# Numpy transposes the first expert matrix, the score keys and the gate matrices before the launch, and the kernel stops transposing them

## The chip, the cores and the metric

The kernel runs on one NeuronCore of a Trainium2 chip. The metric is the device time of one launch in microseconds (us). What numpy does on the host before the launch is not in it. Five engines work beside each other, each in its own fixed order, and wait for one another through semaphores: PE (TensorE: matmuls, and transposes as matmuls against an identity), DVE (VectorE), ACT (ScalarE), POOL (GpSimd) and SP (SyncE, which mostly issues DMAs).

## The reference, cut to what matters

Two layers. Each has a token mixer (attention, mLSTM and a gating MLP side by side) and then a layer of retrieved experts (PEER). There are 512 tokens of width 1024 and 16384 experts per layer.

```python
def spatial_gating(u, v, w_s, b_s):
    ...
    gate = jnp.einsum('gts,bcsgd->bctgd', w_s * tril, v5) + b_s.T[:, :, None]
...
def peer_ffn(xn, wq, sub_keys, u_tab, v_tab):
    q = jnp.matmul(xt, wq).reshape(t, PEER_HEADS, 2, PEER_SUBDIM)
    scores = jnp.einsum('thcd,hcnd->thcn', q, sub_keys)
    sv, si = lax.top_k(scores, PEER_TOPK)
    ...
    best_s, best_p = lax.top_k(cand_s, PEER_TOPK)
    idx = jnp.take_along_axis(cand_i, best_p, axis=-1)
    gate = jax.nn.softmax(best_s, axis=-1)
    ...
        act = jnp.einsum('td,thkd->thk', xb, u_tab[ib])
        wgt = jax.nn.gelu(act) * gb
        return jnp.einsum('thk,thkd->td', wgt, v_tab[ib])
```

`u_tab` and `v_tab` are the kernel's `peer_u` and `peer_v`, [2, 16384, 1024] in float32.

## The kernel before, in words

For the first 384 tokens (TD) the kernel doesn't gather experts. It computes all 16384 activations densely, in 128 blocks of 128 experts: `act = u_block @ x` (`uact`, L733), then gelu, then a product with a sparse gate matrix, then `y += w^T @ v_block` (`vmm`, L989). Each fp32 operand is split into a high and a low fp32r part, and a product is three matmuls (hi*hi, hi*lo, lo*hi). The last 128 tokens are done by gathers: 128 indirect DMAs of rows of `peer_u` and 128 of `peer_v` per layer (`gather_u` L763, `gather_v` L774), each followed by one DVE operation of 128x1024. In these texts a "block" is one such block of 128 experts, and a "gather" is the DVE operation that uses a gathered row.

`uact` needs the block with its 1024 channels on the partitions, but `peer_u` holds it with the experts on them. So each block is loaded (`uload`, L683), transposed and split into `u_hi` (ACT) and `u_lo` (DVE) (`utrans`, L693). There are two ways to transpose. In the first 54 blocks of a layer PE does it: eight 128x128 transposes into two PSUM tiles (L711), each with its own ACT copy (L713) and DVE subtraction (L714) of 128x512. In the other 74 blocks DVE does it: the load comes as four DMAs that place 32-row pieces (L688), one STREAM_TRANSPOSE of 128x1024 finishes it (L702), and ACT and DVE split the whole tile (L705, L706).

A layer runs through these stretches:

- **mixer**, in which four gate matrices are transposed by PE (L550), and **front** (`peer_front`, L618): 16 score projections on PE, each with a key matrix that PE transposes (L648) and ACT copies (L650), and the first top-k on DVE.
- **selection** (`stage2`, L803): the second top-k and the indices of four token tiles on DVE. `paced` (L925) emits a whole block's load, transposes and `uact` for each unit of credit.
- **one-hot** (`onehots`, L895): the sparse gate matrix is built from bf16 one-hot products, DVE 2 `oeq` and 3 `oag` operations per 16 tokens, PE 48 matmuls, ACT four copies. Blocks go on by the same credit, and a gather is emitted at every second step.
- **tail** (L1003 to 1010): 12 blocks and 12 gathers, no other work. Block 51 is its first.
- **dense** (L1014 to 1027): 128 steps of `vmm`, 65 blocks spread between them, the remaining gathers of both kinds.

From the front to the end of the one-hot stretch the Tile scheduler sets the order of each engine when the program is built. The tail and the dense stretch stand in the order in which they are written (`manual_schedule`). The number of blocks in each stretch follows from the credits, which the change doesn't touch: 51 before the tail.

Buffers: three of `u_raw`, two each of `u_hi` and `u_lo`, four for gathered rows, and one PSUM tag `T` with two buffers for the transposes.

## Time and profile before

| | |
|---|---|
| median of 3 runs | 3360.24 us (3348.55 to 3373.12) |
| profiled execution | 3358.58 us, span 3356.9 us, mean granted PE clock 0.986 |
| PE busy | 96% |
| DVE busy | 83% |
| ACT busy | 42% |
| POOL busy | 19% |
| DMA | 742.40 MB, mean 221 GB/s |

The stretches are cut in the trace at these points of layer 0: the front ends when PE has done its last score matmul (L659, 438 us), the one-hot stretch begins with the first `oeq` (L907, 594.1 us) and ends with the last `oag` (L911, 783.8 us), the dense stretch begins with the first `y` matmul (L997, 861 us) and ends with the last (1676.6 us). In layer 1 the same points are 2117.7, 2274.1, 2463.2, 2540.7 and 3352.5 us.

How to read it: a busy share is a mean over a stretch. PE matmuls are pipelined, so a matmul's own duration (341 ns for 384 columns) is longer than the step from its start to the start of the next. What a matmul costs is that step, and it is read from the timeline or from the chain, where a run of equal matmuls has one row with the time to the next piece.

### The profile page before, as it was taken

What the parts mean: (1) busy time and instruction counts of PE and PEld (TensorE: products, weight loads), DVE (VectorE), ACT (ScalarE), POOL (GpSimd) and SP (SyncE); (2) the same over time, 40 slices, a digit from 0 to 9 for tenths busy, and PEclk for the clock granted to TensorE, in tenths of its full rate; (3) what the DMA queues carried; (4) which work ended last, traced back from release to release, by engine and by line L of the source; (5) the groups of instructions that cost most, each with busy time, mean ns of one, the idle gap of its engine ahead of it and who ended that gap; (6) DMA issues with size and microseconds to landing.
All of it is one profiled execution on the core that took longest, in us unless ns stands there. A gap on an engine that the chain in (4) does not pass through costs nothing.

```text
span 3356.9 us, 49064 instructions
## 1 busy us (share of the span) xinstructions
PE 3237.4 (96%) x18400; PEld 2875.2 (86%) x18400; DVE 2792.9 (83%) x4911; ACT 1395.2 (42%) x2142; POOL 652.1 (19%) x563
## 2 busy tenths in 40 slices
PE   8999999999999999999989999999999999999999
PEld 8787899898888888888887778889988888888888
DVE  4757898997888888988847578989978888989888
ACT  4554333664333333333355533336643333333333
POOL 1000003111232232223200000032112222332232
PEclk9999999999999999999999999999999999999999
DMA  4212137777999999999732121377779999999997
GB/s 136 72 33 90 56 121 273 265 282 230 279 296 291 283 292 291 304 297 290 246 112 66 32 90 55 121 271 265 282 233 282 296 289 289 302 301 302 286 290 255
DMA packets 388687, 742.40 MB, mean 221 GB/s; under 512 B 32996, under 2 KB 269600, under 8 KB 385376
## 3 DMA queue, kind: packets, MB, share of 16 engines
q1 hardware_dynamic: 295264, 398.64, 43.1%
q0 software_dynamic: 74752, 269.84, 25.4%
q10 hardware_dynamic: 18432, 70.79, 5.3%
q8 instruction: 144, 2.36, 0.3%
q14 instruction: 95, 0.78, 0.1%
HBM read 666.26 MB, written 72.88 MB: 220 GB/s over the span
## 4 chain that ended last, share of the span: by engine, by line
PE 65%; DVE 13%; DMA 11%; issue 5%; ACT 4%; POOL 1%; SPq 0%; ACTq 0%; DVEq 0%; POOLq 0%
PE y L997 22%; PE act L738 17%; PE mm L187 12%; DMA v_raw<-in_peer_v_dram 8%; PE oh L917 3%; PE mm L533 3%; DVE u_lo L714 2%; DMA u_raw<-in_peer_u_dram 1%; DVE u_t L702 1%; PE T L711 1%; PE zz L367 1%; PE zz L659 1%; PE zz L467 1%; PE y L478 1%; PE y L400 1%
## 5 line engine op out<-in xcount | busy, mean ns | idle before, releaser
L738 PE MATMUL act<-xh,u_lo 128*128 128x384 f32 x2048 | 698.1, 341 | 19.4 <-DVE u_lo L706 19.4
L738 PE MATMUL act<-xh,u_hi 128*128 128x384 f32 x2048 | 705.8, 345 | 11.1 <-ACT u_hi L705 10.7
L738 PE MATMUL act<-xl,u_hi 128*128 128x384 f32 x2048 | 696.7, 340 | 0.0
L997 PE MATMUL y<-v_hi,wh 128*128 128x512 f32 x1536 | 600.0, 391 | 8.8 <-ACT wh L984 8.8
L997 PE MATMUL y<-v_lo,wh 128*128 128x512 f32 x1536 | 600.2, 391 | 1.3 <-DVE v_lo L985 1.2
L997 PE MATMUL y<-v_hi,wl 128*128 128x512 f32 x1536 | 599.2, 390 | 0.0
L983 ACT ACTIVATE v_hi<-v_raw 128x1024 fp32r<-128x1024 f32 x256 | 272.0, 1062 | 742.6 <-DMA v_raw<-in_peer_v_dram 336.0
L985 DVE TENSOR_TENSOR v_lo<-v_raw,v_hi 128x1024 fp32r<-128x1024 f32 x256 | 313.1, 1223 | 146.4 <-ACT v_hi L983 146.2
L738 PEld LDWEIGHTS act<-xh,u_lo 128*128 128x128 f32 x2048 | 388.2, 190 | 26.8 <-DVE u_lo L706 26.8
L738 PEld LDWEIGHTS act<-xh,u_hi 128*128 128x128 f32 x2048 | 388.7, 190 | 24.8 <-ACT u_hi L705 17.3
L738 PEld LDWEIGHTS act<-xl,u_hi 128*128 128x128 f32 x2048 | 388.3, 190 | 4.8
L997 PEld LDWEIGHTS y<-v_hi,wh 128*128 128x128 f32 x1536 | 288.9, 188 | 65.8 <-ACT wh L984 10.7
L997 PEld LDWEIGHTS y<-v_hi,wl 128*128 128x128 f32 x1536 | 289.1, 188 | 62.5 <-DVE wl L986 1.5
L997 PEld LDWEIGHTS y<-v_lo,wh 128*128 128x128 f32 x1536 | 289.0, 188 | 58.0 <-DVE v_lo L985 2.9
L702 DVE STREAM_TRANSPOSE u_t<-u_raw 128x1024 f32<-128x1024 f32 x148 | 327.9, 2215 | 0.1
L765 POOL DMA_INDIRECT rows<-in_peer_u_dram,idx x128 | 150.3, 1174 | 788.1 <-DVE rows L768 412.7
L765 POOL DMA_INDIRECT sbuf<-in_peer_u_dram,idx x128 | 147.8, 1154 | 590.4 <-DVE sbuf L768 468.4
L741 ACT ACTIVATE gelu<-act 128x384 f32<-128x384 f32 x256 | 124.3, 485 | 299.7 <-PE act L738 298.7
L776 POOL DMA_INDIRECT rows<-in_peer_v_dram,idx x128 | 172.4, 1347 | 380.7 <-DVE x_sb L779 355.9
L984 ACT ACTIVATE wh<-wf 128x384 fp32r<-128x384 f32 x256 | 132.7, 518 | 244.9 <-DVE wf L980 244.0
L776 POOL DMA_INDIRECT sbuf<-in_peer_v_dram,idx x128 | 163.5, 1277 | 337.0 <-DVE x_sb L779 313.8
L706 DVE TENSOR_TENSOR u_lo<-u_t,u_hi 128x1024 fp32r<-128x1024 f32 x148 | 181.2, 1224 | 55.5 <-ACT u_hi L705 55.1
(309 smaller groups left out, 5890.1 us busy)
## 6 DMA issues: line engine op xcount, KB each, us to landing
v_raw<-in_peer_v_dram SPq DMA_DIRECT2D x256, 512.0 KB, 12.0
u_raw<-in_peer_u_dram SPq DMA_DIRECT2D x592, 128.0 KB, 11.5
u_raw<-in_peer_u_dram SPq DMA_DIRECT2D x108, 512.0 KB, 4.2
gd<-st ACTq DMA_DIRECT2D x24, 2048.0 KB, 7.3
gt<-gd SPq DMA_DIRECT2D x64, 768.0 KB, 14.0
w_raw<-in_w_in_dram SPq DMA_DIRECT2D x28, 768.0 KB, 4.5
ge<-gelu ACTq DMA_DIRECT2D x104, 192.0 KB, 4.4
gelu_r<-ge SPq DMA_DIRECT2D x104, 192.0 KB, 10.4
```

The lines of the kernel that those rows point to most:

```text
L187: nc.tensor.matmul(ps, a_sel(a[ah], d), b_sel(b[bh], d), start=(d == 0 and i == 0), stop=(d == n - 1 and i == 2))
L533: nc.tensor.matmul(pt, yT[ah][:, b, t * P:(t + 1) * P], wo[bh][:, b, hs], start=(b == 0 and m == 0), stop=(b == n - 1 and m == 2))
L702: nc.vector.transpose(uraw[e].rearrange("p c (g b) -> p g c b", g=4), src.rearrange("p g (f c) -> p g c f", f=32))
L706: nc.vector.tensor_sub(ul, uraw[e], uh.bitcast(F32))
L738: nc.tensor.matmul(pa[:, :TD], a[:, d, :], b[:, d, :TD], start=(d == 0 and i == 0), stop=(d == ND - 1 and i == 2))
L741: nc.scalar.activation(gelu[e], pa[:, :TD], AF.Gelu_apprx_tanh)
L765: nc.gpsimd.indirect_dma_start(out=r, out_offset=None, in_=u_rows, in_offset=bass.IndirectOffsetOnAxis(ap=idx[:, p:p + 1], axis=0))
L776: nc.gpsimd.indirect_dma_start(out=r, out_offset=None, in_=v_rows, in_offset=bass.IndirectOffsetOnAxis(ap=idx[:, p:p + 1], axis=0))
L983: nc.scalar.activation(vh, vraw[e], AF.Copy)
L984: nc.scalar.activation(wh, wf, AF.Copy)
L985: nc.vector.tensor_sub(vl, vraw.pop(e), vh.bitcast(F32))
L997: nc.tensor.matmul(ya[2 * t + half], a[:, tsl], b[:, hs], start=(k == 0 and i == 0), stop=(k == NK - 1 and i == 2))
```

## The change

In `kernel()` numpy makes three arrays before the launch: `sg_w` and `peer_keys` with their last two axes exchanged, in place of the originals, and a new input `peer_ut`, a copy of `peer_u` with each block as [partition f, channel group c, expert n], so that a partition's 1024 values of a block are 4096 contiguous bytes. `peer_u` stays an input, since the gathers read it. In the kernel the identity transposes of blocks, keys and gate matrices go, with the ACT copy of the key. `uload` is one DMA of 512 KB for every block, `utrans` becomes `uprep` (one ACT copy and one DVE subtraction of 128x1024 per block), and the DVE transposes go with the two constants that chose their blocks.

```diff
@@ sg_all
-                    pw = ps.tile([P, S], F32, name="tr", bufs=1)
-                    nc.tensor.transpose(pw[:, :P], wr, ident)
                     wt = tmp("dg", 2, (P, NT, P))[:, 0, :]
-                    nc.vector.tensor_mul(wt, pw[:, :P], upper)
+                    nc.vector.tensor_mul(wt, wr, upper)
@@ peer_front
-                    kr = fr.tile([P, P], F32, name="kr", bufs=2)
-                    nc.sync.dma_start(kr, peer_keys[l, h, which])
-                    pk = ps.tile([P, S], F32, name="zz", bufs=4)
-                    nc.tensor.transpose(pk[:, :P], kr, ident)
-                    kt = fr.tile([P, P], F32, name="kt", bufs=2)
-                    nc.scalar.activation(kt, pk[:, :P], AF.Copy)
+                    kt = fr.tile([P, P], F32, name="kt", bufs=3)
+                    nc.sync.dma_start(kt, peer_keys[l, h, which])
@@ layer
             def uload(e):
-                if e < NK and dve_t(e):
...
-                    for a in range(4):
-                        nc.sync.dma_start(uraw[e][32 * a:32 * (a + 1)], rows[a])
-                elif e < NK:
-                    uraw[e] = pools["up"].tile([P, D], F32, name="u_raw", bufs=3)
-                    nc.sync.dma_start(uraw[e], peer_u[l, e * NK:(e + 1) * NK, :])
-
-            def utrans(e, half, ps, tag="T", **kw):
...
+                if e < NK:
+                    uraw[e] = pools["up"].tile([P, ND, P], F32, name="u_raw", bufs=3)
+                    nc.sync.dma_start(uraw[e], peer_ut[l, e])
+
+            def uprep(e):
+                if e < NK:
+                    uh = pools["up"].tile([P, ND, P], F32R, name="u_hi")
+                    ul = pools["up"].tile([P, ND, P], F32R, name="u_lo")
+                    src = uraw.pop(e)
+                    nc.scalar.activation(uh, src, AF.Copy)
+                    nc.vector.tensor_sub(ul, src, uh.bitcast(F32))
+                    uT[e] = (uh, ul)
@@ uphase
-                utrans(e + 1, 0, ps)
-                utrans(e + 1, 1, ps)
+                uprep(e + 1)
                 uact(e, ps)
@@ tail
-                        utrans(e + 1, 0, ps, f"y{2 * n % 6}")
-                        utrans(e + 1, 1, ps, f"y{(2 * n + 1) % 6}")
+                        uprep(e + 1)
                         gather(G_R)
                         uact(e, ps, bufs=2)
@@ dense
                             uload(eu + 3)
-                            utrans(eu + 1, 0, ps)
                         vprep(k + 1)
                         spread(2 * k, 252)
                         if u_on:
                             uact(eu, ps, bufs=2)
-                            utrans(eu + 1, 1, ps)
+                            uprep(eu + 1)
@@ kernel
+    inputs["sg_w"] = _np.swapaxes(inputs["sg_w"], 2, 3)
+    inputs["peer_keys"] = _np.swapaxes(inputs["peer_keys"], 3, 4)
+    u = _np.asarray(inputs["peer_u"])
+    inputs["peer_ut"] = u.reshape(u.shape[0], NK, NK, P, ND).transpose(0, 1, 3, 4, 2)
```

The scheduler sets new orders from the front to the end of the one-hot stretch, and lines after 50 have other numbers in the changed kernel. Three places on DVE show what moved. `u_lo` is the split of a block, `sbuf,act_g` and `rows,act_g` are gathers (named by their two kinds of buffer), `oeq` and `oag` belong to the one-hot stretch, `idxT`, `gateT` and `gr` are the last steps of the selection.

DVE at the end of the selection, before:

```order
L714 TENSOR_TENSOR u_lo<-T,u_hi 128x512 x2
L768 SCALAR_TENSOR_TENSOR rows,act_g<-rows,xg 128x1024 x2
L768 SCALAR_TENSOR_TENSOR sbuf,act_g<-sbuf,xg 128x1024
L714 TENSOR_TENSOR u_lo<-T,u_hi 128x512 x2
L768 SCALAR_TENSOR_TENSOR sbuf,act_g<-sbuf,xg 128x1024
L768 SCALAR_TENSOR_TENSOR rows,act_g<-rows,xg 128x1024 x2
```

and in the changed kernel:

```order
L840 TENSOR_TENSOR ii<-eq 128x256
L736 SCALAR_TENSOR_TENSOR rows,act_g<-rows,xg 128x1024
L683 TENSOR_TENSOR u_lo<-u_raw,u_hi 128x1024
L736 SCALAR_TENSOR_TENSOR rows,act_g<-rows,xg 128x1024
L736 SCALAR_TENSOR_TENSOR sbuf,act_g<-sbuf,xg 128x1024 x2
L855 CAST idxT<-tr 128x2x128
L857 CAST gateT<-tr 128x128
L683 TENSOR_TENSOR u_lo<-u_raw,u_hi 128x1024
```

The runs of three and four gathers between two blocks are gone. Counted over the selection, DVE's order has 28 gathers and 56 half splits before, 12 gathers and 29 whole splits in the changed kernel. PE's order has 667 `act` matmuls and 216 block transposes there before, 684 and none now.

DVE in the middle of the one-hot stretch, before:

```order
L907 TENSOR_TENSOR oeq<-iota_t,idxT 128x2048 x2
L911 TENSOR_TENSOR oag<-oeq,gateT 128x2048
L768 SCALAR_TENSOR_TENSOR rows,act_g<-rows,xg 128x1024 x2
L911 TENSOR_TENSOR oag<-oeq,gateT 128x2048
L714 TENSOR_TENSOR u_lo<-T,u_hi 128x512 x2
```

and in the changed kernel:

```order
L875 TENSOR_TENSOR oeq<-iota_t,idxT 128x2048 x2
L879 TENSOR_TENSOR oag<-oeq,gateT 128x2048 x3
L736 SCALAR_TENSOR_TENSOR rows,act_g<-rows,xg 128x1024
L683 TENSOR_TENSOR u_lo<-u_raw,u_hi 128x1024
L736 SCALAR_TENSOR_TENSOR rows,act_g<-rows,xg 128x1024
```

Two gathers stand in nearly every step now. Over the whole stretch there are 20 gathers and 44 half splits before, 34 gathers and 22 whole splits in the changed kernel, with the same 48 `oeq` and 72 `oag`. On PE it is 1152 one-hot matmuls, 533 `act` and 176 transposes before, and 1152, 540 and none now. In the tail PE has 312 `act` and 24 transposes before, 288 and none now, and DVE has 12 gathers, 10 STREAM_TRANSPOSE, 10 whole and 8 half splits before, 14 gathers and 13 whole splits now.

DVE in two steps of the dense stretch, before:

```order
L702 STREAM_TRANSPOSE u_t<-u_raw 128x4x8x32
L980 TENSOR_TENSOR wf<-gelu,gt_9079 128x384
L985 TENSOR_TENSOR v_lo<-v_raw,v_hi 128x1024
L986 TENSOR_TENSOR wl<-wf,wh 128x384
L768 SCALAR_TENSOR_TENSOR sbuf,act_g<-sbuf,xg 128x1024
L706 TENSOR_TENSOR u_lo<-u_t,u_hi 128x1024
```

and in the changed kernel:

```order
L948 TENSOR_TENSOR wf<-gelu,gt_8298 128x384
L953 TENSOR_TENSOR v_lo<-v_raw,v_hi 128x1024
L954 TENSOR_TENSOR wl<-wf,wh 128x384
L736 SCALAR_TENSOR_TENSOR sbuf,act_g<-sbuf,xg 128x1024
L683 TENSOR_TENSOR u_lo<-u_raw,u_hi 128x1024
```

Only the STREAM_TRANSPOSE is gone, 64 of them in each layer's dense stretch, and PE's order in it is the same 2304 `y` and 1560 `act` matmuls.

## Rows read from the trace of the kernel before

**Rows 1.** The page, its first part: busy time, share of the span and instructions.

```profile
PE 3237.4 (96%) x18400; PEld 2875.2 (86%) x18400; DVE 2792.9 (83%) x4911; ACT 1395.2 (42%) x2142; POOL 652.1 (19%) x563
```

**Rows 2.** Busy time by stretch: from and to (us), length, then busy us (and instructions) of PE, PEld, DVE, ACT and POOL, granted PE clock, DMA share, GB/s. In each layer the rows are front, selection, one-hot, tail and dense.

```profile
335.00:438.00 103.00, 102.70 (x541) 85.74 (x540) 86.52 (x490) 30.47 (x55) 0.00 (x0) 1.00 0.16 46
438.00:594.10 156.10, 147.45 (x894) 143.13 (x894) 145.25 (x536) 57.98 (x97) 33.66 (x31) 0.99 0.67 228
594.10:783.80 189.70, 184.88 (x1815) 175.00 (x1814) 186.08 (x207) 126.06 (x158) 30.22 (x22) 0.99 0.76 271
783.80:861.00 77.20, 66.05 (x394) 60.32 (x392) 53.22 (x55) 25.13 (x36) 11.15 (x12) 1.00 0.75 212
861.00:1676.60 815.60, 804.19 (x3864) 708.04 (x3864) 717.98 (x782) 283.07 (x384) 243.78 (x194) 0.99 1.03 289
2015.00:2117.70 102.70, 102.39 (x538) 85.47 (x537) 86.55 (x490) 30.48 (x55) 0.00 (x0) 1.00 0.15 46
2117.70:2274.10 156.40, 145.02 (x873) 141.91 (x874) 145.01 (x534) 55.99 (x94) 33.64 (x31) 0.97 0.67 225
2274.10:2463.20 189.10, 186.37 (x1835) 176.54 (x1834) 186.00 (x207) 127.50 (x161) 30.07 (x22) 1.00 0.77 274
2463.20:2540.70 77.50, 66.18 (x394) 60.47 (x392) 53.34 (x55) 25.02 (x36) 11.14 (x12) 1.00 0.73 212
2540.70:3352.50 811.80, 804.19 (x3864) 710.13 (x3864) 717.72 (x781) 284.67 (x384) 240.47 (x193) 0.99 1.02 291
```

**Rows 3.** Groups of instructions by line, shapes kept apart: busy us, mean ns of one, and idle time before them with its releasers.

```profile
L702 DVE STREAM_TRANSPOSE u_t<-u_raw 128x1024 f32<-128x1024 f32 x148 | 327.9, 2215 | 0.1
...
L706 DVE TENSOR_TENSOR u_lo<-u_t,u_hi 128x1024 fp32r<-128x1024 f32 x148 | 181.2, 1224 | 55.5 <-ACT u_hi L705 55.1
...
L714 DVE TENSOR_TENSOR u_lo<-T,u_hi 128x512 fp32r<-128x512 f32 x204 | 131.7, 681 | 15.7 <-ACT u_hi L713 15.5
```

**Rows 4.** The timeline of PE in the one-hot stretch of layer 0: start (us), time of the piece (us), what, and how many in a run.

```profile
603.40 1.11 PE L711 MATMUL T<-ident,u_raw 128*128 128x128 f32 x8
604.27 0.42 PE L738 MATMUL act<-xh,u_lo 128*128 128x384 f32 x1
...
614.98 1.90 PE L917 MATMUL oh<-oag,oeq 128*128 128x128 bf16 x30
616.68 0.42 PE L738 MATMUL act<-xh,u_hi 128*128 128x384 f32 x1
```

**Rows 5.** The chain that ended last, two pieces of the dense stretch: start (us), time (us), what.

```profile
950.63 4.19 PE act L738 x24
954.83 8.17 PE y L997 x36
```

**Rows 6.** The timeline of DVE where the one-hot stretch begins, columns as in Rows 4.

```profile
592.92 1.22 DVE L768 SCALAR_TENSOR_TENSOR rows<-rows,xg 128x1024 f32<-128x1024 f32 x1
...
594.06 2.36 DVE L907 TENSOR_TENSOR oeq<-iota_t,idxT 128x2048 bf16<-128x2048 bf16 x2
596.34 3.49 DVE L911 TENSOR_TENSOR oag<-oeq,gateT 128x2048 bf16<-128x2048 bf16 x3
599.74 1.28 DVE L714 TENSOR_TENSOR u_lo<-T,u_hi 128x512 fp32r<-128x512 f32 x2
600.94 2.35 DVE L907 TENSOR_TENSOR oeq<-iota_t,idxT 128x2048 bf16<-128x2048 bf16 x2
```

**Rows 7.** Busy time of DVE's operation behind a gather (with the short read of its accumulator, so that two instructions are one gather) in the selection and the one-hot stretch of layer 0: length, DVE busy us, clock, DMA share, GB/s.

```profile
438.00:594.10 156.10, 34.16 (x56) 0.99 0.67 228
594.10:783.80 189.70, 23.76 (x42) 0.99 0.76 271
```

**Rows 8.** Three windows with the columns of Rows 2: two at the end of the selection, one in the tail of layer 0.

```profile
545.00:570.00 25.00, 23.35 (x144) 22.57 (x142) 20.89 (x37) 6.91 (x13) 11.86 (x11) 1.00 0.91 323
570.00:595.00 25.00, 22.00 (x122) 20.78 (x121) 18.82 (x34) 6.24 (x11) 11.99 (x10) 0.93 0.96 346
...
845.00:870.00 25.00, 19.16 (x88) 16.02 (x87) 18.16 (x23) 8.42 (x11) 3.98 (x4) 0.93 1.05 268
```

**Rows 9.** What DVE waited for from 545 to 595 us: us in total, times, longest.

```profile
DVE rows L768 <- DMA rows<-in_peer_u_dram,idx: 6.2, 6, 2.1
...
DVE sbuf L768 <- DMA sbuf<-in_peer_u_dram,idx: 4.1, 5, 1.6
```

**Rows 10.** Who waited for whom in the dense stretch of layer 0, the rows of PE: us in total, times, longest.

```profile
PE act L738 <- DVE u_lo L706: 6.3, 5, 1.7
...
PE y L997 <- ACT wh L984: 5.1, 3, 3.7
...
PE act L738 <- ACT u_hi L705: 2.8, 3, 1.3
```

**Rows 11.** The hardware DMA queue that SP issues to, from 435 to 580 us, where its block loads are 4 KB rows: packets, MB, share of 16 engines.

```profile
q1 hardware_dynamic: 3744, 13.63, 29.9%
```

**Rows 12.** The same queue from 950 to 1650 us, in the dense stretch, and two of its loads there (KB each, median us from issue to landing).

```profile
q1 hardware_dynamic: 95936, 116.18, 63.7%
...
v_raw<-in_peer_v_dram SPq DMA_DIRECT2D x108, 512.0 KB, 12.4
u_raw<-in_peer_u_dram SPq DMA_DIRECT2D x218, 128.0 KB, 12.1
```

**Rows 13.** One matmul form over the whole execution: least, median and longest duration in ns, first and last start in us.

```profile
L738 PE MATMUL act<-xl,u_hi x2048: 332/338/669, 439.9 to 3315.2; 128*128 128x384 f32 x187
```

40 lines of the change are left out of this document (6 added, 34 removed).

## The prediction

> **What bounds the kernel now.** I read the page first: PE is busy for 96% of the span and DVE for 83% [rows 1]. Two engines that full can each set the end, in different stretches, and a mean over the span doesn't say which. So the second view is the busy time by stretch [rows 2]. In the front PE has no gap (102.70 of 103.00 us, DVE 86.52). In the selection both are nearly full (PE 147.45, DVE 145.25 of 156.10), and in the one-hot stretch too (184.88 and 186.08 of 189.70). In the tail neither is (66.05 and 53.22 of 77.20), so they wait for each other there. In the dense stretch PE has 804.19 of 815.60 us, DVE 717.98, and the DMA share is 1.03. Layer 1 repeats all five.
>
> The third view is the step of each kind of work. On PE, eight block transposes take 0.87 us from start to the next piece, 0.11 each; 30 one-hot matmuls take 1.70, 0.057 each [rows 4]; 24 `act` matmuls, one block, take 4.19, or 0.175 each, and 36 `y` matmuls, two steps, 8.17 [rows 5]. On DVE two half splits take 1.20 us, two `oeq` 2.28, three `oag` 3.40, and an operation of 128x1024 1.14 [rows 6]; a gather with its accumulator is 34.16/28 = 1.22 in the selection and 23.76/20 = 1.19 in the one-hot stretch [rows 7]. A whole split and a gather operation have nearly one duration, so I take 1.14 for the split; the transposes of DVE last 2.215 each [rows 3].
>
> **The dense floor.** 128 steps are 64 x 8.17 = 523 us and 65 blocks are 65 x 4.19 = 272: 795 us of PE that the change leaves alone. Measured are 815.6 and 811.8 [rows 2], so at most 20 and 16 can go there. Most of the kernel is therefore fixed, and the gain has to come from what lies before.
>
> **The change, part by part, for layer 0.**
>
> Front and mixer: 16 key transposes and 4 gate transposes leave PE, which is full in the front: 20 x 0.11 = 2.2 us, with the first block's transposes at the border some 2.4. The keys' ACT copies cost nothing, ACT having 30.47 of 103 us to do [rows 2]. The loads of the keys now end in the tile that the matmul reads, and have three buffers; I take no wait for them, since SP could issue each one block of scores earlier than it is needed. Ends: 0 and 3.
>
> Selection: PE loses 216 transposes (24 us) and has 684 x 0.175 = 120 us left. That isn't the gain, because DVE is full beside it. DVE loses 16 gathers (16 x 1.22 = 19.5) which the scheduler moves to later stretches, and 56 x 0.60 = 33.6 us of half splits become 29 x 1.14 = 33.1: 145.25 - 20 = 125 us. DVE's 10.9 us of idle time are almost all in the last 50 us (20.89 and 18.82 of 25 [rows 8]), where it waits 10.3 us for gathered rows to land [rows 9] because the gathers stand there in runs of three and four. Fewer of them leave half of that, 5 us. I take 130 us, 26 less. Ends: 125 (no wait) and 137 (all the wait, and 1 for the closer race of PE and DVE).
>
> One-hot: the gathers come back here, and DVE already sets the pace. 14 more cost 14 x 1.19 = 16.7 us; 44 x 0.60 = 26.4 of half splits become 22 x 1.14 = 25.1. So 186.1 + 16.7 - 1.3 = 201.5, and with the idle time of before (3.6, of which I keep 2.5) 204 us: 14 **more**. PE has 1152 x 0.057 + 540 x 0.175 = 160 us and some 8 of changes between the two kinds, far below. Ends: 200 and 212.
>
> Tail: PE's 66.05 busy us lose 24 transposes and 24 `act` (2.6 + 4.2), so 59. The 11 us of waiting stood behind a chain of 2.2 us of DVE transpose, an ACT copy and 1.2 us of split [rows 3], beside a gather for each block; without the 10 transposes DVE has 13 x 1.14 + 14 x 1.22 = 32 us for 59 of PE. I keep 2 us of waits: 61, so 16 less. Ends: 59 and 70, the second if the same loads, pressed into fewer us, land late: 212 GB/s x 77/61 is 268, below the 289 that the dense stretch carries [rows 2].
>
> Dense: of the 20 us above the floor, 9.1 are PE's waits for `u_lo` and `u_hi` and 5.1 for `wh` [rows 10]. The chain to `u_lo` loses its first 2.2 us, DVE loses 64 x 2.215 = 142 of 718 us, and the loads get lighter: the queue's engine time per MB is 0.299 x 145 x 16 / 13.63 = 51 us with 4 KB rows [rows 11] and 0.637 x 700 x 16 / 116.18 = 61 in the dense stretch [rows 12]; on 218 x 128 KB = 28.6 MB that is 290 of 11200 engine-us, 2.6 points of DMA share out of 103. Landings of 12 us [rows 12] against 12.4 us for two steps and a block show why that matters. I take half of the 20: 10 less. Ends: 0 and 20. The Trainium skill, on the page "DMA: Bandwidth & Descriptors", table at its head, puts the least transfer for line rate at 512 B; by that rule 1 KB pieces cost no more per byte than 4 KB rows. Rows 11 and 12 speak against it, if mildly, since the dense queue also carries 512 B pieces of the gate matrix. By the rule the dense stretch would give 7, and the sum would be 3285.
>
> Sum: -2.4 - 26 + 14 - 16 - 10 = -40.4. For layer 1 the same from 156.4, 189.1, 77.5 and 811.8: -2.4 - 26.4 + 14.9 - 16.5 - 9 = -39.4. The profiled execution took 3358.6 us with what lies around its span, 1.6 below the median of the runs shown. 3358.6 - 79.8 = 3279.
>
> The 864 block transposes are 95 us of PE and the 148 of DVE 328 us, so the sum of what is removed is five times what I expect. The difference is hidden: by DVE before the dense stretch, by PE in it.
>
> **The rivals.**
>
> *Both floors are reached.* If no wait is left, the stretches are 125, 200, 59 and 795: per layer about -60, in all 3358.6 - 119 = 3240. For it: a block no longer passes through PE, or twice through DVE, on its way to its matmuls. Against: two buffers of `u_hi`, and gathers that still stand in DVE's fixed order. Chance 0.14.
>
> *The waits only move.* `u_hi` is now one ACT copy of a whole tile, and `u_lo` waits for all of it, where halves overlapped before; behind a waiting `u_lo` stand DVE's one-hot operations, and PE waits for these. If 0.23 us per block is lost so in 51 blocks, 12 us, then selection and one-hot keep their 346 us, and if DMA alone holds the dense stretch it keeps its 815.6. What is left is front and tail: 2 x 18.6, so 3321. For it: DVE does wait for ACT there now (15.5 us before the half splits [rows 3]). Against: ACT is busy for a third of the selection [rows 2]. Chance 0.14, and 0.08 for something between it and no change.
>
> *PE falls to its low clock.* Granted are 0.99 and 1.00 in the one-hot stretches with PE almost full [rows 2]; where PE had 22.0 and 19.2 of 25 us the clock was 0.93 [rows 8]. Now PE has 168 us of work in 204, in bursts. At the low level, 1.2 GHz, an `act` matmul lasts 669 ns against 338 [rows 13], so all of PE's work doubles. The mechanism decides once the mean clock is below 168/204 = 0.82; PE then sets the pace, runs full, and the rows show a full PE getting its clock back. To be slower by 1% in all, each layer must lose 57 us more than forecast, a one-hot stretch of 261 us, mean clock 0.64, and 3393 us. The Trainium skill, page "TensorE: Matmul & The Clock Gate", section "A second HAM failure mode: psum-queue depth-cycling", says that small idle times between groups of matmuls are enough to make the clock swing; the windows of rows 8 swing so, but shallowly. Chance 0.04.
>
> That the change doesn't do what it says I rule out: the last two axes of `peer_ut` are 8 x 128 floats, 4 KB in a row per partition, so no strided read takes the transposes' place.
>
> **How the numbers follow.** The forecast has 0.60, with its own range of 3262 to 3300 from half the ends of its terms. The range that holds 8 in 10 takes in most of both neighbours: 3238 to 3322. A measurement of this kernel can tell about 1%, 34 us; faster by more than that is below 3327. Forecast, floors and most of "the waits only move" lie there: 0.87. Within 1%: 0.09. Slower: 0.04.
>
> **What would show it.** Right: no PE work between the last score matmul and the first `act`; selection near 130 us; the one-hot stretch *longer* than before, with DVE full and PE near 85%; the tail near 61 with PE almost without gaps; `y` and `act` steps still 8.17 and 4.19, DVE below 590 us of busy time in the dense stretch, and its DMA share near 1.0. Wrong: a dense stretch that stays above 810 (then loads hold it, and the block chain never did), a one-hot stretch below 195 (then DVE wasn't its bound), or a granted clock below 0.9 in it.

## The result and the profile after

The changed kernel takes 3266.70 us (median of 4 runs, 3263.36 to 3270.06) against 3363.49 (4 runs, 3348.55 to 3373.12: the three that stand before the prediction and one more): a ratio of 0.9716, 95% interval 0.9677 to 0.9755. Forecast were 3279 us, 3238 to 3322. The profiled execution took 3270.06 us, span 3268.4, mean granted clock 0.984 (0.986 before).

Busy time by stretch after the change, with the columns and the order of [rows 2]:

```profile
347.30:444.30 97.00, 96.22 (x490) 79.36 (x490) 85.93 (x489) 26.87 (x38) 0.00 (x0) 1.00 0.15 48
444.30:572.70 128.40, 122.27 (x683) 119.56 (x683) 124.49 (x476) 53.05 (x69) 21.70 (x16) 0.99 0.61 203
572.70:774.70 202.00, 177.55 (x1661) 161.45 (x1661) 200.56 (x212) 123.96 (x140) 57.29 (x35) 0.98 0.78 293
774.70:833.70 59.00, 52.98 (x331) 52.36 (x330) 32.76 (x43) 21.72 (x29) 14.60 (x14) 0.99 0.86 301
833.70:1632.00 798.30, 798.25 (x3864) 706.38 (x3864) 587.95 (x717) 283.97 (x384) 227.62 (x193) 1.00 0.87 294
1975.70:2072.80 97.10, 96.31 (x491) 79.43 (x490) 85.91 (x489) 26.88 (x39) 0.00 (x0) 1.00 0.15 48
2072.80:2202.90 130.10, 122.45 (x683) 119.72 (x683) 124.52 (x476) 53.98 (x70) 21.51 (x16) 0.99 0.63 204
2202.90:2404.90 202.00, 178.88 (x1661) 163.10 (x1662) 200.54 (x212) 123.03 (x138) 57.22 (x35) 0.97 0.77 291
2404.90:2464.80 59.90, 53.99 (x331) 53.41 (x330) 32.73 (x43) 21.89 (x29) 14.60 (x14) 0.96 0.86 301
2464.80:3263.40 798.60, 798.49 (x3864) 706.55 (x3864) 587.98 (x718) 283.95 (x384) 226.01 (x192) 1.00 0.88 295
```

Cut at the same points, the two profiled executions differ so:

| us, layer 0 / layer 1 | before | after | difference | forecast |
|---|---|---|---|---|
| mixer | 337.7 / 340.9 | 347.3 / 343.7 | +9.6 / +2.8 | with the front |
| front | 100.3 / 100.2 | 97.0 / 97.1 | -3.3 / -3.1 | -2.4 / -2.4 |
| selection | 156.1 / 156.4 | 128.4 / 130.1 | -27.7 / -26.3 | -26 / -26.4 |
| one-hot | 189.8 / 189.1 | 202.0 / 202.0 | +12.2 / +12.9 | +14 / +14.9 |
| tail | 77.1 / 77.4 | 59.0 / 59.9 | -18.1 / -17.5 | -16 / -16.5 |
| dense | 815.6 / 811.8 | 798.4 / 798.6 | -17.2 / -13.2 | -10 / -9 |

In the one-hot stretch DVE is busy for 200.56 of 202.00 us and sets the pace. In the dense stretch PE has no gap left (798.25 of 798.30). Before, it had 11.4 us of gaps, and the same matmuls took 5.9 us more (804.19) at a granted clock of 0.99. These two are the whole 17 us. Two of the signs that I set out didn't come: the DMA share there is 0.87, where I wrote "near 1.0", and in the tail PE has gaps for 6.0 of 59.0 us, where I wrote "almost without gaps".

The mixer is longer, but it varies from one profile to the next: over the twelve profiles with the new gate layout 339.1 to 347.3 us in layer 0 and 338.5 to 346.7 in layer 1, with the same code in it. It goes with the granted clock. Layer 0's mixer before, after, and in one of the later kernels with the new layout (transposes, whole loads), columns as in [rows 2]:

```profile
0.00:337.70 337.70, 315.55 (x1721) 265.29 (x1721) 207.59 (x395) 172.43 (x340) 16.90 (x43) 0.98 0.27 82
0.00:347.30 347.30, 322.64 (x1722) 270.91 (x1722) 209.14 (x396) 173.29 (x340) 16.89 (x43) 0.96 0.27 83
0.00:339.10 339.10, 316.05 (x1721) 265.74 (x1721) 208.65 (x396) 173.39 (x340) 16.91 (x43) 0.98 0.27 85
```

So 7.1 of layer 0's 9.6 us are PE's own time at a lower clock, and at the clock of before the new layout costs 1.4 us more. Why the clock differs from one execution to the next, these runs don't show. In layer 1 the clock is 0.95 in both, and whether its 2.8 us belong to the change isn't settled.

### The profile page after: what moved, and what is told of

Same layout as the page of the kernel before. It is cut to its first block, busy times and chain, and to the rows that moved or that the text cites. A ratio compares the mean times of both kernels' runs of the same rounds, so it can differ in the third digit from the quotient of the medians.

```text
span 3268.4 us, 46257 instructions
## 1 busy us (share of the span) xinstructions
PE 3139.1 (96%) x17496; PEld 2780.4 (85%) x17496; DVE 2481.4 (76%) x4655; ACT 1371.0 (42%) x2002; POOL 658.5 (20%) x563
## 4 chain that ended last, share of the span: by engine, by line
PE 63%; DVE 8%; ACT 2%; issue 1%; DMA 1%; POOL 0%; SPq 0%; ACTq 0%; POOLq 0%; DVEq 0%
PE y L965 32%; PE act L707 20%; PE mm L185 6%; DVE oag L879 2%; PE mm L531 1%; DVE u_lo L683 1%; DMA v_raw<-in_peer_v_dram 1%; DVE oeq L875 1%; DVE rows L736 1%; ACT st L888 1%; DVE sbuf L736 1%; PE zz L365 1%; PE zz L651 0%; PE oh L885 0%; PE zz L465 0%
## 5 line engine op out<-in xcount | busy, mean ns | idle before, releaser
L707 PE MATMUL act<-xh,u_hi 128*128 128x384 f32 x2048 | 694.8, 339 | 16.0 <-ACT gelu L710 11.4
L707 PE MATMUL act<-xh,u_lo 128*128 128x384 f32 x2048 | 696.3, 340 | 12.7 <-DVE u_lo L683 12.3
L683 DVE TENSOR_TENSOR u_lo<-u_raw,u_hi 128x1024 fp32r<-128x1024 f32 x256 | 312.8, 1222 | 268.8 <-ACT u_hi L682 266.0
L682 ACT ACTIVATE u_hi<-u_raw 128x1024 fp32r<-128x1024 f32 x256 | 270.7, 1057 | 180.4 <-PE act L707 169.6
L733 POOL DMA_INDIRECT rows<-in_peer_u_dram,idx x128 | 169.9, 1328 | 681.4 <-DVE c L794 353.6
L733 POOL DMA_INDIRECT sbuf<-in_peer_u_dram,idx x128 | 164.6, 1286 | 581.8 <-DVE sbuf L736 461.2
L744 POOL DMA_INDIRECT rows<-in_peer_v_dram,idx x128 | 155.4, 1214 | 381.5 <-DVE x_sb L747 357.0
L888 ACT ACTIVATE st<-oh 128x512 f32<-128x512 f32 x192 | 192.7, 1148 | 94.4 <-PE oh L885 91.8
L744 POOL DMA_INDIRECT sbuf<-in_peer_v_dram,idx x128 | 150.4, 1175 | 348.1 <-DVE x_sb L747 328.8
```

What stands on the lines that cost most here:

```text
L682: nc.scalar.activation(uh, src, AF.Copy)
L683: nc.vector.tensor_sub(ul, src, uh.bitcast(F32))
L707: nc.tensor.matmul(pa[:, :TD], a[:, d, :], b[:, d, :TD], start=(d == 0 and i == 0), stop=(d == ND - 1 and i == 2))
L733: nc.gpsimd.indirect_dma_start(out=r, out_offset=None, in_=u_rows, in_offset=bass.IndirectOffsetOnAxis(ap=idx[:, p:p + 1], axis=0))
L744: nc.gpsimd.indirect_dma_start(out=r, out_offset=None, in_=v_rows, in_offset=bass.IndirectOffsetOnAxis(ap=idx[:, p:p + 1], axis=0))
L888: nc.scalar.activation(st[:, :, o:o + 4].rearrange("p i t -> p t i"), pg, AF.Copy)
```

## The experiments

Stretches are layer 0 / layer 1 of one profile; each ratio is against the kernel before on the same chip. Its median was 3361.35 us beside the first four kernels after "after", and 3350.44 and 3355.18 beside the later ones, so the ratios of two rows compare better than their medians.

| kernel | median us | ratio, 95% interval | selection | one-hot | tail | dense |
|---|---|---|---|---|---|---|
| before | 3363.49 | | 156.1 / 156.4 | 189.8 / 189.1 | 77.1 / 77.4 | 815.6 / 811.8 |
| after | 3266.70 | 0.9716, 0.9677 to 0.9755 | 128.4 / 130.1 | 202.0 / 202.0 | 59.0 / 59.9 | 798.4 / 798.6 |
| blocks only | 3263.42 | 0.9728, 0.9686 to 0.977 | 126.6 / 126.6 | 202.0 / 202.0 | 57.8 / 58.8 | 797.4 / 798.1 |
| keys and gates only | 3353.78 | 0.9983, 0.9961 to 1.0005 | 156.7 / 155.0 | 189.7 / 189.0 | 77.1 / 77.9 | 809.4 / 816.1 |
| early blocks (PE's) | 3312.78 | 0.9864, 0.982 to 0.9908 | 129.1 / 128.9 | 202.0 / 202.0 | 72.8 / 74.1 | 815.7 / 814.5 |
| late blocks (DVE's) | 3303.63 | 0.9845, 0.9804 to 0.9887 | 156.2 / 156.6 | 189.1 / 189.0 | 67.0 / 65.7 | 798.7 / 797.7 |
| 1 KB loads for all | 3343.65 | 0.9995, 0.9969 to 1.002 | 121.5 / 121.9 | 231.5 / 230.1 | 66.2 / 68.8 | 807.9 / 801.2 |
| spare transposes | 3265.40 | 0.9754, 0.9722 to 0.9786 | 128.4 / 128.9 | 202.0 / 201.9 | 59.6 / 57.8 | 797.7 / 796.4 |
| 1 KB loads, late blocks | 3292.50 | 0.9824, 0.9782 to 0.9866 | 127.9 / 129.2 | 202.1 / 202.0 | 66.0 / 70.1 | 805.3 / 797.3 |
| transposes, whole loads | 3293.64 | 0.982, 0.9785 to 0.9855 | 128.6 / 129.5 | 202.0 / 201.9 | 73.1 / 72.9 | 797.6 / 797.4 |
| more blocks early | 3214.31 | 0.9598, 0.9567 to 0.963 | 128.2 / 128.1 | 215.0 / 215.0 | 20.5 / 20.8 | 796.4 / 799.7 |
| gathers late | 3224.05 | 0.9623, 0.9591 to 0.9656 | 124.3 / 123.3 | 183.5 / 183.5 | 59.3 / 61.0 | 801.2 / 800.6 |
| both of these | 3206.15 | 0.956, 0.9526 to 0.9595 | 122.9 / 123.3 | 212.5 / 212.5 | 20.6 / 21.5 | 800.3 / 802.4 |
| both, some gathers kept | 3207.68 | 0.9564, 0.953 to 0.9598 | 128.6 / 129.0 | 210.1 / 210.1 | 21.0 / 20.5 | 799.9 / 799.8 |

### The parts alone

**Blocks only** gives the gates and the keys back to PE:

```diff
+                    pw = ps.tile([P, S], F32, name="tr", bufs=1)
+                    nc.tensor.transpose(pw[:, :P], wr, ident)
...
+                    nc.tensor.transpose(pk[:, :P], kr, ident)
+                    kt = fr.tile([P, P], F32, name="kt", bufs=2)
+                    nc.scalar.activation(kt, pk[:, :P], AF.Copy)
...
-    inputs["sg_w"] = _np.swapaxes(inputs["sg_w"], 2, 3)
-    inputs["peer_keys"] = _np.swapaxes(inputs["peer_keys"], 3, 4)
```

> The changed kernel with the key and gate transposes put back on PE; only the blocks come transposed. My theory (each stretch gains by its own bound): the blocks carry the whole gain but about 5 us, so about 3272 us, ratio 0.973 to before; the front is 100 us long as before, the selection 128, the one-hot stretch 202, the tail 59, the dense stretch 798. Rival A (PE's removed work is the gain, wherever it stands): the 40 transposes put back cost 40 x 0.11 = 4.4 us, the same time. Rival B (the mixer lost 6 us in layer 0 through the host-transposed gates and keys): the mixer of layer 0 ends at 338 instead of 347 us, and the time is 3262.

**Keys and gates only** is the reverse, the kernel before with these two layouts alone.

> The kernel before with only the keys and gate matrices transposed by numpy. My theory: 20 transposes per layer leave PE where it is full, 2.4 us per layer, 3358 us (0.9985): no change that can be told; front 98 us. Rival B: the mixer of layer 0 gets 6 to 10 us longer and the time stays at 3363 or goes up to 3370. Rival A: 4.4 us less.

**Early blocks** takes the first 54 blocks of a layer from numpy's copy and leaves the other 74 to DVE and their four-piece loads; **late blocks** does the opposite:

```diff
+            def host_t(e):
+                return not dve_t(e)     # late blocks: return dve_t(e)
```

> Keys, gates and the first 54 blocks of a layer from the transposed copy, the other 74 still transposed by DVE with their loads in 1 KB pieces. My theory: selection 128 and one-hot 202 us as in the changed kernel, together 16 less than before, tail about 74, dense stretch 812 to 816 as before: 3358.6 - 2 x 18 = 3323 us (0.988). Rival A (the removed PE work is the gain): all 95 us of transposes are gone, so 3270 us (0.972), as in the changed kernel. Rival C (the loads of 1 KB pieces are the whole cost in the dense stretch): dense as before.

> Keys, gates and the 74 late blocks from the transposed copy, the first 54 still transposed by PE. My theory: selection 156 and one-hot 190 us as before, tail 62, dense 798: 15 + 15 us per layer and 2 for keys, 3358.6 - 64 = 3295 us (0.980). Rival A: DVE's transposes were hidden under a full PE, so at most the tail gains, 3330 us (0.990).

Keys and gates are worth nothing that can be measured: 0.9983, with 1 inside the interval. Their front gets 1.6 us shorter in each layer (98.7 against 100.3). So all that counts is in the blocks, and blocks only shows it: 0.9728 against 0.9716 for the whole change. It took 3263.42 us, where I expected 3272 and rival B, by the mixer, 3262. But its mixer of layer 0, with the old layouts, is 340.9 us long at a clock of 0.97, and those of early and late blocks, with the new ones, 341.7 and 341.3; the layout isn't what lengthens it.

The gain of the blocks falls apart by place: PE's blocks give the selection and cost the one-hot stretch, DVE's blocks give the dense stretch. The tail takes some of each (3 to 4 us by the early blocks, 10 to 12 by the late ones, 18 by both). The two ratios multiply to 0.971, the ratio of the change. The single forecasts were off: early blocks took 3312.78 us where 3323 was expected, late blocks 3303.63 where it was 3295. In the late blocks' tail (67.0 and 65.7, expected 62) PE still has the transposes of three blocks and the `act` matmuls of a thirteenth, 394 instructions as before, and is busy for 62.50 of 67.00 us.

### Loads or transposes: the dense stretch

The late blocks lost two things at once: DVE's transpose, and loads in 1 KB pieces. I had taken half of what could go, without knowing which of the two held it.

**1 KB loads for all** loads every block of the changed kernel by four DMAs, as the late blocks were before:

```diff
+                    for a in range(4):
+                        nc.sync.dma_start(uraw[e].rearrange("p (g i) n -> p g (i n)", g=4)[32 * a:32 * (a + 1)],
+                                          peer_ut[l, e, :, 32 * a:32 * (a + 1), :].rearrange("g p c -> p g c"))
```

> The changed kernel with each block load cut as the late blocks' loads were before: four DMAs of 32 partitions in pieces of 1 KB (numpy lays peer_ut out so that the pieces lie apart). No transposes anywhere. Theory D (the dense stretch was held by its loads): dense goes back up to 808 to 816 us, and the time to about 3295. Theory E (it was held by the chain load, DVE transpose, ACT copy, split, and by DVE's load): dense stays at 798 to 801 us, 3265 to 3275. The DMA share in the dense stretch should go back from 0.87 to about 0.93 or more in both.

This run separates less than was meant. The whole gain is gone (0.9995), but most of it in stages that the edit reordered: with other DMAs the scheduler moved blocks from the selection to the one-hot stretch, which grew to 231.5 us.

```profile
438.00:559.60 121.60, 91.05 (x470) 84.06 (x468) 116.47 (x470) 41.84 (x52) 24.16 (x17) 0.96 0.59 170
559.60:791.10 231.50, 206.45 (x1844) 195.10 (x1845) 210.74 (x219) 135.04 (x152) 54.39 (x35) 0.97 0.88 280
```

PE's instructions in the two stretches were 683 and 1661 after the change; here they are 470 and 1844. Neither engine fills the longer stretch, and PE waits 20.7 us there for `u_lo`. So neither theory's time came (3295, or 3265 to 3275; measured 3343.65). What it says of loads alone is left to its dense stretch, and that doesn't decide either: 807.9 in layer 0, the lower end of theory D, and 801.2 in layer 1, the upper end of theory E. The next runs leave the early order as it is.

**Spare transposes** puts DVE's load back without its place in the chain: 64 transposes per dense stretch whose result nothing reads.

```diff
+                    if extra:
+                        junk = pools["up"].tile([P, ND, P], F32, name="u_t", bufs=1)
+                        nc.vector.transpose(junk.rearrange("p c (g b) -> p g c b", g=4),
+                                            src.rearrange("p c n -> p (c n)").rearrange(
+                                                "p (g f c) -> p g c f", g=4, f=32))
```

> The changed kernel with a DVE transpose of 128x1024 added behind each split of the dense stretch, into a tile that nobody reads (64 per layer, 2.2 us each): DVE's load is as before, the chain to the matmul isn't, and the loads are large. Theory E1 (DVE's load was the cause): dense 808 to 816 us. Theory E2 (the transpose in the chain was the cause): dense 798 to 802. Theory D (the loads): 798 to 802. DVE busy in the dense stretch about 718 us.

Its two dense stretches:

```profile
831.50:1629.30 797.80, 797.39 (x3864) 706.13 (x3864) 711.01 (x781) 294.22 (x384) 269.48 (x193) 1.00 0.86 295
2457.30:3253.80 796.50, 796.05 (x3864) 705.06 (x3864) 710.89 (x782) 294.22 (x384) 261.62 (x192) 1.00 0.87 297
```

DVE is as busy as before the change (711 us against 718) and the stretch stays at 797. The 142 us of DVE time that the change removes are worth nothing by themselves.

**1 KB loads, late blocks** and **transposes, whole loads** then complete a table of two by two, and keep the order of all earlier stages. The first loads blocks 54 to 127 in 1 KB pieces from a copy arranged for it, without a transpose; the second loads them whole and keeps DVE's transpose in the chain:

```diff
-                    nc.sync.dma_start(uraw[e], peer_ut[l, e])
+                    if e < LATE:
+                        nc.sync.dma_start(uraw[e], peer_ut[l, e])
+                        return
...
+                    for a in range(4):
+                        nc.sync.dma_start(uraw[e].rearrange("p (g i) n -> p g (i n)", g=4)[32 * a:32 * (a + 1)],
+                                          cut[32 * a:32 * (a + 1)])
```

```diff
+                elif e < NK and dve_t(e):
+                    uraw[e] = pools["up"].tile([P, 4, ND * 32], F32, name="u_raw", bufs=3)
+                    nc.sync.dma_start(uraw[e], peer_ut[l, e].rearrange("p c n -> p (c n)").rearrange(
+                        "p (g c) -> p g c", g=4))
```

> The changed kernel, but blocks 54 to 127 of each layer are loaded as four DMAs of 1 KB pieces (as the kernel before loads them), out of a copy that numpy arranged so; nothing is transposed on the chip, and the stages before the tail are those of the changed kernel. Loads theory (the dense stretch of the kernel before stood at 812 to 816 us because its loads took more of the DMA engines' time): dense 810 to 816 us in both layers, DMA share near 1.0, whole kernel 3290 to 3300. Chain theory (it stood there because u_lo came late, behind a transpose of 2.2 us on DVE, an ACT copy and a subtraction): dense stays at 797 to 800 us, whole kernel 3266. Selection 128, one-hot 202 and tail 59 us are expected unchanged by both; a tail of 66 or more would say that the tail too was held by loads.

> The other half: blocks 54 to 127 are loaded whole, in 4 KB rows, out of a copy that numpy arranged so that DVE's transpose of 2.2 us still has to be made on the chip, between the load and the ACT copy. DVE has the work of the kernel before in the dense stretch, the loads are those of the changed kernel. Loads theory: dense 797 to 800 us, DMA share near 0.88, although DVE is busy for some 715 us of it. Chain theory: dense 810 to 816 us. The tail: 59 to 62 us if its waits came from the loads, 72 to 74 (as with 1 KB pieces and the transpose) if they came from the chain on DVE. Whole kernel 3267 with the loads theory in both places, 3295 with loads in dense and chain in the tail, 3330 with the chain in both.

| dense, layer 0 / layer 1 (us) | no transpose | transpose in the chain |
|---|---|---|
| whole loads (4 KB rows) | 798.4 / 798.6 | 797.6 / 797.4 |
| 1 KB pieces | 805.3 / 797.3 | 815.7 / 814.5 |

The chain theory falls for the dense stretch: with whole loads the transposes cost nothing (797 us in both layers, as with the spare ones). The small loads are what the lost time can't do without. Alone they cost 7 us in one layer of the profile and nothing in the other, which is less than the loads theory said, and with the transposes 16 to 17 in each.

Whether both together cost more than the loads alone is likely, but not shown. For it: over all profiles the dense stretch with pieces and transposes is 809.4 to 816.1 us (six layers: before, keys and gates only, early blocks), with pieces alone 797.3 to 807.9 (four: this run and 1 KB loads for all), and with whole loads 796.4 to 798.7 in the five kernels that keep the gathers in their places. Against it: the profiled execution of early blocks (3323.07 us) is the slowest of its four and that of 1 KB loads for all (3332.31) the fastest of its ten. By the medians the loads alone cost 26 us against the changed kernel, the transposes alone 27, both 46; less the two tails (17, 27 and 28, next paragraphs) the dense stretches are left with 9, 0 and 18. By the ratios the three cost 36, 35 and 50 us, and 19, 8 and 22 are left; the 8 where the profile shows no loss tells how far such sums can be trusted. So the size of that step stays open.

Two things besides the size of a piece differ in the lower row of the table. A load in pieces is four DMAs of 32 partitions in place of one of 128, and no run separates the two. And with the transposes the pieces are quarters of the 4 KB rows of `peer_u`, while without them numpy has laid 32 of them side by side.

The dense windows of the three, 1 KB loads first, then transposes with whole loads, then both (which is the early blocks kernel):

```profile
839.80:1645.10 805.30, 800.56 (x3864) 707.69 (x3864) 587.92 (x717) 283.41 (x384) 232.27 (x193) 0.99 0.98 292
2487.00:3284.30 797.30, 797.23 (x3864) 705.65 (x3864) 587.86 (x717) 284.17 (x384) 225.81 (x192) 1.00 0.98 295
```

```profile
839.80:1637.30 797.50, 797.33 (x3864) 706.06 (x3864) 718.70 (x781) 285.55 (x385) 228.56 (x194) 1.00 0.88 294
2485.30:3282.70 797.40, 797.18 (x3864) 705.93 (x3864) 718.76 (x781) 285.57 (x385) 228.49 (x193) 1.00 0.88 295
```

```profile
842.50:1658.20 815.70, 804.71 (x3864) 710.70 (x3864) 718.50 (x781) 284.30 (x385) 238.37 (x194) 0.99 1.01 288
2502.30:3316.80 814.50, 805.94 (x3864) 708.39 (x3864) 717.96 (x781) 283.63 (x385) 248.16 (x192) 0.99 1.01 289
```

With the pieces the DMA share is 0.98 and 1.01, against 0.88, and the loads land later. What is late for its reader is not the blocks themselves but the loads of the second matrix, which share the engines. The row of ACT's wait for them, in the dense stretch of layer 0: before the change, in the early blocks kernel, with 1 KB loads alone, and after the change (us in total, times, longest). With whole loads and transposes there is no such row.

```profile
ACT v_hi L983 <- DMA v_raw<-in_peer_v_dram: 210.5, 51, 9.2
```

```profile
ACT v_hi L989 <- DMA v_raw<-in_peer_v_dram: 121.5, 28, 12.7
```

```profile
ACT v_hi L958 <- DMA v_raw<-in_peer_v_dram: 39.0, 9, 7.8
```

```profile
ACT v_hi L951 <- DMA v_raw<-in_peer_v_dram: 2.7, 1, 2.7
```

How a late `v_raw` reaches PE is seen in the one disturbance of the run with 1 KB loads alone: ACT's timeline in layer 0 (start, time, what, then the idle time before it and what ended it), the load of `v_raw` that ACT's third row reads (its issue on SP, then its size and its time from issue to landing), and the two waits of PE that follow.

```profile
1211.04 0.53 ACT L959 ACTIVATE wh<-wf 128x384 fp32r<-128x384 f32 x1 [0.23 <-DVE wf L955]
1222.14 1.06 ACT L958 ACTIVATE v_hi<-v_raw 128x1024 fp32r<-128x1024 f32 x1 [10.58 <-PE y L972]
1223.11 0.51 ACT L959 ACTIVATE wh<-wf 128x384 fp32r<-128x384 f32 x1
1223.52 0.47 ACT L717 ACTIVATE gelu<-act 128x384 f32<-128x384 f32 x1
1223.89 1.04 ACT L689 ACTIVATE u_hi<-u_raw 128x1024 fp32r<-128x1024 f32 x1
```

```profile
1203.98 6.22 SPq L944 DMA_DIRECT2D v_raw<-in_peer_v_dram  x1
```

```profile
v_raw<-in_peer_v_dram SPq DMA_DIRECT2D x1, 512.0 KB, 18.1
```

```profile
1224.99 0.45 PE L714 MATMUL act<-xh,u_hi 128*128 128x384 f32 x1 [2.96 <-ACT u_hi L689]
1227.31 0.66 PE L714 MATMUL act<-xh,u_lo 128*128 128x384 f32 x1 [1.70 <-DVE u_lo L690]
```

ACT stands 10.58 us in front of `v_hi`. The row names PE as the releaser, since a step of `y` ended in the same moment. But `v_hi` has two buffers, and the step that frees this one had ended by 1213.8 us. The load landed 18.1 us after its issue at 1203.98, at 1222.0, and `v_hi` starts at 1222.14: the load was late. Behind `v_hi`, in ACT's fixed order, stand `wh`, a `gelu` and the next `u_hi`, and PE stops for `u_hi` and then for `u_lo`. The block's own load isn't named in either wait. PE's 4.7 us of gaps come with a dip of the granted clock, in three windows of 10 us:

```profile
1210.00:1220.00 10.00, 10.00 (x51) 9.02 (x50) 4.06 (x6) 1.34 (x2) 1.95 (x2) 1.00 1.05 333
1220.00:1230.00 10.00, 5.34 (x19) 4.32 (x19) 7.01 (x9) 4.26 (x6) 2.95 (x2) 0.87 0.56 159
1230.00:1240.00 10.00, 10.00 (x47) 8.77 (x47) 5.16 (x8) 2.91 (x4) 2.27 (x2) 0.96 1.07 338
```

In the kernel before, such a delay met a block chain longer by 2.2 us, on a DVE busy for 88% of the stretch. If the transposes do add to a delay, whether by the longer chain or by the fuller DVE these runs don't tell: 1 KB loads with spare transposes would, and that wasn't tried.

In the **tail** each cause costs time alone, the chain more than the loads, so that loads in the dense stretch and the chain in the tail make the 3295 us that were set out for that case (3293.64 measured): 66.0 and 70.1 us with the pieces, 73.1 and 72.9 with the transposes, 72.8 and 74.1 with both, 59 to 60 with neither. With the pieces alone much of it is the first step of `y`, for which PE waits 8.8 and 12.7 us in the two layers, 4.1 and 4.7 after the change. With the transposes it is the chain itself: with whole loads, ACT waits 39.4 us of 73.2 for DVE's transposes, and PE behind it for both parts of a block (us in total, times, longest):

```profile
ACT u_hi L711 <- DVE u_t L708: 39.4, 10, 4.5
...
PE act L744 <- DVE u_lo L712: 5.4, 9, 0.7
...
PE act L744 <- ACT u_hi L711: 2.6, 8, 0.5
```

### What the new shape allows

If DVE sets the one-hot stretch and the tail is PE's, two constants of the schedule should be worth something that they weren't before. **More blocks early** raises the credit for blocks in the one-hot stretch (`W_O` from 0.5 to 0.75), **gathers late** takes the gathers out of it (`G_B` from 1 to 0), the next does both, and the last leaves one gather in every fourth place:

```diff
-W_O = 0.5
+W_O = 0.75
...
-G_B = 1
+G_B = 0
```

```diff
-                        gather(G_B * (n % 2))
+                        gather(G_B * (n % 4 == 3))
```

> The changed kernel with the one-hot stretch's credit at 0.75 instead of 0.5 per two steps, so that 9 of the 12 tail blocks are emitted there. My theory: DVE sets the one-hot stretch and PE has 24 us to spare there; 9 to 10 splits of 1.14 us and 2 gathers lengthen it by 13 to 20 us (PE then needs 1152 x 0.057 + 756 x 0.175 + 10 = 208 us), the tail shrinks from 59 to about 18, the dense stretch takes 9 more gathers without cost: 25 us per layer less than the changed kernel, 3217 us (0.957). Rival: PE and DVE, both full at 215 us, wait for each other as before the change, the stretch grows by 35 us, and nothing is left: 3260.

> The changed kernel with no gathers emitted in the one-hot stretch: the 48 of each layer go to the dense stretch, where DVE has 210 us to spare. My theory: selection 128 - 12 x 1.22 = 113 to 120 us (PE needs 116), one-hot 202 - 34 x 1.19 = 162 to 172 us (PE needs 168), dense 798 if the DMA share (0.87, now plus 48 x 0.5 MB on 234 MB, about 0.95) leaves the loads in time: 40 us per layer less, 3185 us (0.948). Rival: the dense stretch, with a tenth more DMA traffic and DVE at 640 us, gets the waits of before back, 812 us: 3215 (0.957).

> The changed kernel with two constants of its schedule moved at once: half as many blocks again in the one-hot stretch (12 more out of the tail), and no gather interleaved there. Each alone gave 3214 and 3224. PE has 1152 x 0.057 + 779 x 0.175 = 202 us and some 10 of changes there, DVE some 176. If the two act on different limits, PE sets a one-hot stretch of 210 to 214 us, the tail stays near 20 and the kernel comes to 3190 to 3205. If the gathers that leave the one-hot stretch hold the tail or the dense stretch instead (dense 801 us with the gathers late), nothing is won over 3214.

> As the last, but with one gather in every fourth place of the one-hot stretch in place of none. DVE has some 186 us there and PE some 208, so PE still sets it: one-hot 207 to 212 us, tail 20, dense 796 to 800 (half of the gathers that were moved to it are back), 3190 to 3205. Against it: if DVE and PE wait for each other whenever both are near full, one-hot stays at 215 and the kernel at 3214.

The one-hot stretch of layer 0 with gathers late, with more blocks early, with both, and with some gathers kept:

```profile
563.00:746.50 183.50, 177.35 (x1692) 160.44 (x1691) 163.48 (x145) 122.41 (x140) 0.00 (x0) 1.00 0.61 221
```

```profile
572.10:787.10 215.00, 205.64 (x1877) 192.38 (x1876) 214.12 (x225) 137.95 (x158) 68.18 (x37) 1.00 0.85 307
787.10:807.70 20.60, 16.76 (x116) 16.26 (x115) 7.99 (x12) 9.10 (x12) 2.88 (x3) 0.92 0.75 269
```

```profile
564.20:776.80 212.60, 208.80 (x1910) 198.45 (x1909) 175.92 (x155) 139.70 (x160) 0.00 (x0) 1.00 0.60 218
797.30:1597.70 800.40, 799.60 (x3864) 705.48 (x3864) 651.86 (x831) 287.11 (x385) 307.42 (x250) 1.00 0.94 332
```

```profile
569.90:780.10 210.20, 203.99 (x1874) 192.73 (x1875) 187.84 (x178) 137.61 (x158) 22.50 (x13) 1.00 0.71 254
```

Without gathers DVE drops from 200.56 to 163.48 busy us, and the stretch follows only to 183.50, where PE is nearly full. That shows DVE as the bound before, and PE 18 us behind it. The kernel missed its forecast, 3224.05 us against 3185, since PE was taken 9 us too low there (168 us, measured 177.35), the selection fell to 124 and not to 113 to 120, and the dense stretch, at a DMA share of 0.93, grew by 2 to 3 us per layer. The 812 us of its rival didn't come. More blocks early came to 3214.31 for 3217; they cost 13.0 us of one-hot and save 38.5 of tail: there nine more blocks no longer stand between a load and a wait, but beside DVE's work, where PE had 24 us to spare. Together they gain little over the first alone, and the last two kernels stay 1 to 3 us above the range set out for them: PE sets the one-hot stretch (208.80 of 212.60), and with all gathers pushed into it the dense stretch has 2 to 4 us more per layer, at a DMA share of 0.94. With 3206.15 and 3207.68 us these two have the lowest medians, below both kernels of this study: 1.6% below the changed one by their ratios (0.956 / 0.9716 = 0.984). The ratios of the last four overlap at their edges, so an order among them isn't claimed.

## Why the prediction was right, and where its terms were off

**Front.** Forecast -2.4, measured -3.3 and -3.1. Half of it is the keys' (98.7 with keys and gates only), the other half the first block's transposes, for which I had 0.2. After the last score matmul the next work on PE is the first `act`, as written. The keys' loads held nothing.

**Selection.** Forecast 130, measured 128.4 and 130.1. The sum was DVE's: 125 busy us were forecast, 124.49 measured, by 16 fewer gathers (24 instructions for 12 gathers, where [rows 7] have 56 for 28). The waits for gathered rows in the last 50 us, 10.3 before [rows 9], are these two after:

```profile
DVE rows L736 <- DMA rows<-in_peer_u_dram,idx: 1.1, 1, 1.1
DVE sbuf L736 <- DMA sbuf<-in_peer_u_dram,idx: 0.7, 1, 0.7
```

I kept 5 of the 10.3; 1.8 are left. PE and DVE race more closely instead (122.27 and 124.49 of 128.40). How closely shows in the gathers late run, whose selection has no gathers at all:

```profile
438.60:563.00 124.40, 117.56 (x651) 115.42 (x650) 110.33 (x450) 51.12 (x66) 4.02 (x4) 0.97 0.51 164
```

DVE has 14 us less to do and the stretch is 4 us shorter, with PE now the fuller engine. So the sum of DVE alone came out right with little to spare; PE's floor stood right behind it.

**One-hot.** Forecast 204 and "longer", measured 202.0 in both layers, with DVE at 200.56 (forecast 201.5) and PE at 88% of the stretch (85 forecast). The gathers late run shows that DVE was the bound, as the term assumed. This is the term that a count of removed work would have given the wrong sign.

**Tail.** Forecast 61, measured 59.0 and 59.9. The chain of transpose, copy and split was the right cause, shown by the run that puts it back (73). But that the sum is so near is luck: PE was to be busy for 59 us and is for 52.98, and 2 us of waits were to be left and 6.0 are. I had taken the removed matmuls off PE's 66.05 busy us, which held matmuls drawn out by the waits between them: with the transposes in the chain 330 instructions take PE 59.39 us, without them 331 take 52.98. What PE still waits for is not a block; its two longest waits stand at the ends of the stretch, the first step of `y` and the last copy of the one-hot stretch (`st`):

```profile
PE y L965 <- ACT wh L952: 4.1, 1, 4.1
...
PE act L707 <- ACT st L888: 1.9, 1, 1.9
```

The second bound, late loads, turned out real as well (66 to 70) but didn't occur, because the loads had become lighter by more than I reckoned.

**Dense.** Forecast -10 and -9 ("I take half of the 20"), measured -17.2 and -13.2. The direction and the floor were right: 795 us of steps [rows 5], 798.3 measured. The size was off. I kept half of the waits without a row that said which half, and the step that failed is the one on the loads: "2.6 points of DMA share out of 103". Measured are 16 points. The hardware queue of SP over the dense stretch of layer 0, before and after (packets, MB, share of 16 engines):

```profile
q1 hardware_dynamic: 109419, 133.02, 62.5%
```

```profile
q1 hardware_dynamic: 82605, 132.93, 50.0%
```

The same bytes take 12.5 points less. The error is the price of a 1 KB piece. I took 61 engine-us per MB, but that is the mean of the whole queue, with its 4 KB rows and its 512 B pieces. By the DMA records of this stretch the 31748 pieces of 1 KB took 76.1 ns each on average, 74 engine-us per MB, and the 4 KB rows after the change take 187.7 ns, 46 per MB. On the blocks' 32.5 MB that is 927 engine-us, 7 points where I had 2.6. The queue as a whole went from 8157 to 6385 engine-us, so 845 of the 1772 saved belong to transfers that the change doesn't touch: they got shorter too, the other 4 KB rows from 208.5 to 187.7 ns and the 512 B pieces from 35.5 to 29.1. For these I had no term. With whole loads next to nothing above the floor of 795 us was left, whatever DVE did (796.4 to 798.7 us).

By the Trainium skill's 512 B for line rate ("DMA: Bandwidth & Descriptors", section "Specifications") 1 KB pieces would have cost nothing more. The 12.5 points, and the 9.3 of the run with 1 KB loads alone (59.3% against 50.0%), speak against it for this queue. Another sentence of the Trainium skill agrees with the runs: "Perfetto Trace Analysis", section "DMA Optimizations", sets the overhead per transfer as significant below 2 KB.

My test for the dense stretch, "a dense stretch that stays above 810 (then loads hold it, and the block chain never did)", wasn't called on, since both went at once. By the later runs its second half is right for the chain alone with whole loads, and the 5.1 + 9.1 us of PE's waits that I divided between `wh` and the block [rows 10] need not be two prices: in the one disturbance followed through, ACT was late at `v_hi`, with `wh` and `u_hi` both behind it.

**The rivals.** *Both floors* came closest: the stretches besides the mixer give -101.3 in all against the forecast's -79.8 and this rival's -119. The mixer's +12.4 brought the total back to -88.9 in the profiles, so that the predicted 3279 is only 9 us off the 3270 of the profiled execution is partly luck: two errors, 21.5 less and 12.4 more, cancel in part. The 12.4 had no term at all; 7 of them go with the clock in layer 0's mixer. *The waits only move* didn't happen: selection and one-hot together fell from 345.9 to 330.4 us. *PE at its low clock* didn't either: granted are 0.98 and 0.97 in the one-hot stretches, though PE is in bursts there; with 177.55 busy us and 24 of gaps that stayed far from 0.64.

## What to carry to other kernels

Read every stretch by the engine that fills it, and follow removed work to what takes its place: of 95 + 328 us of transposes about a fifth came back, and one stretch grew. The mean of a queue isn't the price of one kind of transfer in it: read that kind's own records, and expect the others to get shorter with it (927 and 845 engine-us here, where 290 were reckoned). And where a change removes two suspected causes of one wait, put each back alone before either is given a price: here the 142 us of DVE work were worth nothing in the dense stretch by themselves, and without the small loads no time was lost there.
